# First pointwise product of a Conformer layer: eight column groups advanced together with the adaLN slices, and most of the depthwise convolution placed behind them

## The chip, the cores and the metric

The kernel runs on one core of a Trainium2 chip. The metric is device time in microseconds (us), the median of three runs. A core has a matrix engine (PE, TensorE), a vector engine (DVE), a scalar engine (ACT), a general engine (POOL) and a queue engine (SP) that here issues nearly every DMA. They run side by side, each in its own program order, and wait for each other by semaphores.

## The reference, cut to what matters

Two layers over x of 256 tokens by 2048 channels, all in 32-bit floats. Layer 0 mixes tokens by a Conformer convolution, layer 1 by differential attention, and each is followed by a squared-ReLU MLP (2048 to 8192 to 2048). Only the beginning of layer 0 is touched:

```
mod = silu(c) @ ada_w[0] + ada_b[0]         # (2048) @ (2048, 6 * 2048): sh_m, sc_m, g_m, sh_f, sc_f, g_f
h = x * (1 + sc_m) + sh_m
u = h @ pw1_w + b1                          # (256, 2048) @ (2048, 4096)
u = u[:, :2048] * sigmoid(u[:, 2048:])      # GLU
u = causal depthwise convolution of u, width 31, + b_dw
u = silu(layer_norm(u))                     # over the 2048 channels
y = u @ pw2_w + b2                          # (256, 2048) @ (2048, 2048)
x = layer_norm(alpha * x + g_m * y)
...
```

The channel h[:, k] needs sc_m[k] and sh_m[k], so the first product can't begin its contraction before the modulation vectors are there, and each of those six vectors costs the reading of a 2048 by 2048 block of ada_w (16 MB).

## The kernel before

**Products.** A product takes three PE matmuls for each 128 rows of contraction ("kc", 16 of them), 128 tokens and 512 columns: both operands are split into a high and a low part, and high x high, high x low and low x high are added in PSUM (`mm_parts`, L480; L488 to L490, and L563 to L566 in the later products). A weight tile of 1 MB is loaded, then split in two halves of 128x1024 each: ACT writes the high part (L476, L527), DVE the low part (L477, L528; a few on POOL). One half feeds 12 matmuls. PSUM has eight banks of 128x512: four for products (`mm_bank`), three for transposes and small things (`tp_tile`), one for the adaLN products.

**adaLN vectors.** There are two ways to compute one. The DVE way (`ada_slice_dve_steps`, L222) multiplies each row block of a loaded 1 MB tile with one column of silu(c) and adds it up (L248); matmuls with a vector of ones (L231) sum over the partitions. The PE way (`ada_slice_steps`, L264) multiplies on PE (L289; eight short matmuls for a 1 MB tile), copies, transposes (L272) and reduces. A step is one 1 MB tile.

**First part, L870 to L1001.** sc_m (DVE way) and sh_m (PE way) are computed in five slices of the 2048 channels, `SLICES` = 2, 4, 4, 4 and 2 blocks of 128. When a slice is there, h is transposed, scaled and split for its channels (`end_ada`, L934), and the first product advances over these kc for four of its eight column groups (a group is 512 columns: 256 of the value half and 256 of the gate half). Groups 0 and 1 (`RES`) stay in four PSUM banks for the whole time. Groups 2 and 3 (`ROT`) use rotating banks, and `add_up` (L942) adds each slice to a sum in SBUF. In between `ada_pair` works off one step of each kind for the next slice and loads two more tiles. PE, DVE, ACT and SP follow the order of the code here.

**Second part, L1055 to L1085.** Groups 4 to 7 run one after the other over all 16 kc (eight halves each). After each half `run_plan` issues what is due of the convolution: for each group j `glu` (L796), `conv_shift` (L742: 16 copies into a buffer in which the 31 taps become a contraction), `conv_taps`, `conv_products` (L763: 64 short matmuls for each of two channel blocks), `conv_out`, `conv_tok` and `conv_stats`. The convolution of groups 0 to 6 lies in this part; that of group 7 comes behind it. 24 of the 32 DVE steps for G_M and SC_F (8 channel blocks each) are spread over the 32 halves, with tiles loaded ahead (`dve_loads`).

**Third part, L1087 to L1138.** Group 7's convolution, PE steps of SH_F (`fill`), channel LayerNorm, swish.

**Fourth part, the second pointwise product "pw2"** (`out_proj`, L1202): 16 weight tiles. After each `pump_t2` (L1183) works off the remaining 8 DVE steps and the remaining PE steps of the 16 for SH_F. The PE steps' tiles are loaded ahead (`load_pe`, L376). For these last 8 DVE steps no load was issued ahead: `step` (L251) finds no tile and issues the load itself, right in front of its own arithmetic. DVE follows the order of the code from here on too (`early_ve`), and so its splits of the weights (L528) queue behind these steps. Then comes the MLP of layer 0.

Tiles for adaLN live in a pool of two buffers (`araw`), in halves of the buffer `ux`, and in the first part in two of the four buffers of the weight tiles (`ada_raw`, L193).

Of the kernel before, what the change touches and what calls it, by code (L numbers as in the profile page):

```python
# [19 lines left out]
P = 128  # L20
# [10 lines left out]
RES = (0, 1)  # L31
ROT = (2, 3)
ACC0 = 2
SLICES = ((0, 2), (2, 4), (6, 4), (10, 4), (14, 2))
ADA_T1 = 24
FILL = (2, 1, 1, 2)
# [17 lines left out]
OV_AT = 1  # L54
SUM_WAIT = 4
# [4 lines left out]
SHIFT = ("act", "act", "act", "dve")  # L60
END_ACT = (0, 3, 6, 9, 12, 15)
CONV_AT = (4, 8, 12, 16, 20, 24, 28)
# [16 lines left out]
def trunk(  # L79
# [68 lines left out]
    small_rows = {}  # L148

    def load_small(n, name, vs):  # L150
        o = 0
        for v in vs:
            r = vec_rows(v)
            nc.sync.dma_start(vtok[o:o + r.shape[0], 1, n * P:(n + 1) * P], r)
            o += r.shape[0]
        small_rows[name] = vtok[:o, 1, n * P:(n + 1) * P]
# [36 lines left out]
    def ada_raw(name, first):  # L193
        if pe_turn[0] > 0:
            if pe_turn[0] % 3 == 0:
                return ux[:, 2048:]
        elif first:
            n_raw[0] += 1
            n = n_raw[0] % 6
            if n in (2, 3):  # L200
                return ux[:, (n - 2) * 2048:(n - 1) * 2048]
            if n in (4, 5):
                return wraw.tile([P, 2048], F32, tag="raw", name=name)
        return araw.tile([P, 2048], F32, tag="araw", name=name)

    n_raw, pe_turn = [0], [0]
    ux = big.tile([P, 4096], F32, tag="uTh", name="conv_ux")

    def slice_tiles(i, v, f0, nf, first):

        n0, w = (v * KC + f0) * P, nf * P
        per = 2048 // w
        av = ada_w[i].rearrange("(kc p) n -> p kc n", p=P)

        def load(a):
            t = ada_raw(f"aw_{i}_{v}_{f0}_{a}", first)
            tv = t.rearrange("p (j n) -> p j n", n=w)
            nc.sync.dma_start(tv, av[:, per * a:per * (a + 1), n0:n0 + w])
            return tv
        return load, per, w  # L220

    def ada_slice_dve_steps(i, v, f0, nf, m, first=True):  # L222
# [3 lines left out]
        load, per, w = slice_tiles(i, v, f0, nf, first)  # L226
# [37 lines left out]
    def ada_slice_steps(i, v, f0, nf, m, first=False, apart=False):  # L264

        st = {}
        load, per, w = slice_tiles(i, v, f0, nf, first)
# [74 lines left out]
    ada_q, dve_loads, dve_q, pe_q = [], [], [], []  # L342

    def add_dve(v, f0, m):
        loads, steps = ada_slice_dve_steps(0, v, f0, 8, m, False)
        dve_loads.extend(loads)
        dve_q.extend(steps)
    m_gm, m_scf, m_shf = mod_tile(0, G_M), mod_tile(0, SC_F), mod_tile(0, SH_F)
    add_dve(G_M, 0, m_gm)
    add_dve(G_M, 8, m_gm)  # L350
    add_dve(SC_F, 0, m_scf)
    add_dve(SC_F, 8, m_scf)
    pe_loads = []
    for f0 in range(0, KC, 4):
        loads, steps = ada_slice_steps(0, SH_F, f0, 4, m_shf, apart=True)
        pe_loads.extend(loads)
        pe_q.extend(steps)
# [10 lines left out]

    def pump_early(q, n=1):
        for _ in range(n):  # L370
            if q:
                q.pop(0)()
                if q is pe_q:
                    load_pe()

    def load_pe():  # L376
        if pe_loads:
            pe_turn[0] = 1 - pe_turn[0]
            pe_loads.pop(0)()
            pe_turn[0] = -pe_turn[0]  # L380
# [350 lines left out]
    xs_buf = [ux[:, 0:4 * 2 * UW], econv.tile([P, 4 * 2 * UW], F32, name="conv_x")]  # L731
# [8 lines left out]
    turn = {j: n for n, j in enumerate(ROT + RES + tuple(range(len(RES + ROT), 8)))}  # L740

    def conv_shift(j, bs=range(4)):  # L742

        u = cs[j]["u"].rearrange("p n s -> p (n s)")
        for b in bs:
            for r in range(4):
                dst, src = xs_buf[turn[j] % 2][32 * r:32 * r + 32, b, :XW], u[32 * b:32 * b + 32, r:r + XW]
                if (4 * b + r in END_ACT) if j == 7 else SHIFT[(r - b) % 4] == "act":
                    nc.scalar.copy(dst, src)
                else:  # L750
                    nc.vector.tensor_copy(dst, src)

    def conv_taps(j, n):
        cs[j]["dg", n] = []
        for hb in range(2):
            w = work.tile([P, 16, 32], F32, tag="CB"[n], name=f"conv_w_{j}_{n}_{hb}")
# [6 lines left out]
    def conv_products(j, n):  # L763
        cs[j]["ps", n] = ps = tp_tile(f"cv_{j}_{n}")
        for k4 in range(8):
            for b in range(4):
                nc.tensor.matmul(ps[32 * b:32 * b + 32, :S], lhsT=cs[j]["dg", n][k4 // 4][:, (k4 % 4) * 4 + b, :],
                                 rhs=xs_buf[turn[j] % 2][:, b, n * UW + 4 * k4:n * UW + 4 * k4 + S],
# [20 lines left out]
    def glu_copy(j, pss):  # L789
        cs[j]["ut"] = []  # L790
        for t in range(NT):
            u_t = work.tile([P, NG], F32, tag="A", name=f"utok_{j}_{t}")
            nc.scalar.copy(u_t, pss[t])
            cs[j]["ut"].append(u_t)

    def glu(j):  # L796
        ut = cs[j]["ut"]
        if turn[j] < len(u_buf):
            u = u_buf[turn[j]]
        else:  # L800
            u = work.tile([P, 2, UW], F32, tag="X", name=f"u_{j}", bufs=3)
        cs[j]["u"] = u
        pa = tp_tile(f"pa_{j}")
        pg = tp_tile(f"pg_{j}")
# [21 lines left out]
    pss0 = {g: [mm_bank(f"pw1_{g}_ps{t}") for t in range(NT)] for g in RES}  # L826
    accs = {g: [vtok[:, t, (ACC0 + r) * NG:(ACC0 + r + 1) * NG] for t in range(NT)] for r, g in enumerate(ROT)}
# [53 lines left out]
    order = [ROT + RES if nf == 2 else tuple(g for gs in zip(ROT, RES) for g in gs) for f0, nf in SLICES]  # L881
    n_first = len(RES + ROT)
    w_src = [(f"pw1_{g}_{s}", pw1v[:, f0:f0 + nf, :, g * 256:(g + 4 // nf) * 256])
             for s, (f0, nf) in enumerate(SLICES) for g in order[s][::4 // nf]]
    w_src += [(f"pw1_{g}_{i}", pw1v[:, i:i + 4, :, g * 256:(g + 1) * 256])
              for g in range(n_first, 8) for i in range(0, KC, 4)]
# [47 lines left out]
    def end_ada(s):  # L934
        f0, nf = SLICES[s]
        for f in ada_end[s]:
            f()
        nc.vector.tensor_scalar(mul[:, f0:f0 + nf], m_sc[:, f0:f0 + nf], 1.0, None, ALU.add)
        to_featT(z, hT, mul, m_sh, "h0", range(f0 // 2, (f0 + nf) // 2))()
        later.extend([lambda q=q: alpha_x(q) for q in range(f0 // 4, (f0 + nf) // 4)])  # L940

    def add_up(g, s, pss):  # L942
        for t in range(NT):
            if s == 0:
                nc.scalar.copy(accs[g][t], pss[t])
            else:
                nc.vector.tensor_tensor(accs[g][t], accs[g][t], pss[t], op=ALU.add)
# [5 lines left out]
    for _ in range(2):  # L953
        load_w()
    for _ in range(2):
        ada_load.pop(0)()
# [9 lines left out]
    for s, (f0, nf) in enumerate(SLICES):  # L966
        last = f0 + nf == KC
        n_half = nf // 2 * n_first
        nxt = 0 if last else len(ada_step[s + 1])
        pair_at = {4: (0, 1, 2, 3) if n_half == 4 else (1, 3, 5, 7), 2: (2, 4), 0: ()}[nxt]  # L970
        h = 0
        for n, g in enumerate(order[s]):
            pss = pss0[g] if g in RES else [tp_tile(f"pw1_{g}_{s}_ps{t}") for t in range(NT)]
            k0, k1 = (0, KC - 1) if g in RES else (f0, f0 + nf - 1)
            for q in range(nf // 2):
                split_half()
                mm_parts(pss, hT, w_parts.pop(0), f0 + 2 * q, k0, k1)
                pending()
                if h in pair_at:
                    ada_pair(s + 1)  # L980
                if nxt and h == (5 if nxt == 2 else n_half - 1):
                    pending()
                    end_ada(s + 1)
                h += 1
            if g in ROT:
                later.append(lambda g=g, s=s, pss=pss: add_up(g, s, pss))
                cs[g]["ut"] = accs[g]
                if nf == 2:
                    pending()
            if last and n == 2:  # L990
                glu(ROT[0])
                glu_copy(RES[0], pss0[RES[0]])
        if s == CV_AT:
            conv_vectors()
        if s == OV_AT:
            load_small(1, "adab1", [ada_b[1]])
            load_small(2, "b1", [mlp_b1[0], mlp_b1[1]])
        if s == OV_AT + 1:
            load_small(3, "ln", [ln_mix_g[0], ln_mix_b[0], ln_ffn_g[0], ln_ffn_b[0], ln_mix_g[1], ln_mix_b[1]])
            load_small(0, "subg", [attn_subln_g[0]])  # L1000
    pending()  # L1001
# [22 lines left out]
    pairs = sorted(turn, key=turn.get)  # L1024
    for n, c in enumerate(CONV_AT):
        for e in range(2):
            at(c + 2 * e + 2, conv_tok, pairs[n], e)
            at(c + 2 * e, conv_products, pairs[n], e)
    at(1, glu, pairs[1])
    at(5, glu, pairs[2])  # L1030
    at(9, glu, pairs[3])
    at(13, glu, pairs[4])
    at(17, glu, pairs[5])
    at(25, glu, pairs[6])
    for n, c in enumerate(CONV_AT):
        for e in range(2):
            at(c + 2 * e + 1, conv_out, pairs[n], e)
            at(max(0, c + 2 * e - 3), conv_taps, pairs[n], e)
            at(c + 2 * e + 3, conv_stats, pairs[n], e)
        for b in range(4):  # L1040
            at(c - 4 + b if n < 6 else (c - 3, c - 2, c - 2, c - 1)[b], conv_shift, pairs[n], [b])
    pw1 = {}
    at(6, lambda: glu_copy(pairs[3], pss0[pairs[3]]))
    at(10, lambda: glu_copy(4, pw1[4]))
# [550 lines left out]
```

## Time and profile before

| | |
|---|---|
| median of 3 runs | 2450.39 us (2448.82 to 2453.74) |
| profiled execution: time | 2448.23 us |
| profiled execution: span from first to last instruction | 2446.4 us |
| PE busy / DVE busy / ACT busy | 2302.1 / 1764.3 / 1064.3 us |
| mean granted PE clock | 0.97 |
| bytes moved by DMA | 608.5 MB |
| first matmul of pw1 / last matmul of pw1 | 33.0 / 359.5 us |
| first matmul of pw2 / last matmul of pw2 | 398.6 / 532.5 us |
| first matmul of the MLP | 547.0 us |

How to read the lines: a row of the stretches ("windows") gives start and end, its length, the busy time of PE, PE's weight loads, DVE, ACT and POOL with the number of instructions, and then the granted PE clock (1.00 is full), the DMA share and GB/s. A row of the groups gives line, engine, operation, tiles, shapes and count, then busy us and mean ns of one, and then the idle time before them and what ended it. A row of the waits gives who waited for whom, us in total, times, longest. A row of the timeline gives start and duration. PE matmuls overlap, so that the pace of PE is the distance between two starts, not the duration of one, and a "busy" PE can be a slow one.

### The profile page before, as it was taken

The numbers are of one execution on the slowest core, as the hardware profiler recorded it, in microseconds if no ns is written. First come the engines' busy times: TensorE is split into PE (matmuls) and PEld (weight loads), VectorE is DVE, ScalarE is ACT, GpSimd is POOL, SyncE is SP. The second block draws the span as 40 slices with busy tenths as digits, with TensorE's granted clock in tenths as the row PEclk, the third lists the DMA queues.
The fourth block names the chain that finished last, engine by engine and source line by source line (L and its number), as shares of the span: only waits on it lengthen the run. The fifth ranks groups of instructions, "written<-read, shape, count | busy, mean of one in ns | idle before, by whom it ended". The sixth has DMA issues, their size and how long they took to land.

```text
span 2446.4 us, 28510 instructions
## 1 busy us (share of the span) xinstructions
PE 2302.1 (94%) x11167; PEld 1829.7 (75%) x11167; DVE 1764.3 (72%) x1988; ACT 1064.3 (44%) x1370; POOL 245.7 (10%) x162
## 2 busy tenths in 40 slices
PE   4898988789999999999998999998999999999997
PEld 2666664567778888888886888886788888888886
DVE  5667873578898878878868777787877665565566
ACT  2336654234434434434435454444543443443442
POOL 0000000122060000000004300012204000000002
PEclk9889998899999999999998999999999999999999
DMA  9976776667889888888874676686686555556563
GB/s 350 349 249 235 256 249 249 231 241 262 323 301 330 288 318 303 293 311 306 302 257 160 228 243 222 227 288 211 217 286 217 188 189 189 191 188 194 185 223 103
DMA packets 274027, 608.53 MB, mean 249 GB/s; under 512 B 11038, under 2 KB 48484, under 8 KB 260580
## 3 DMA queue, kind: packets, MB, share of 16 engines
q1 hardware_dynamic: 273652, 606.41, 72.0%
q8 instruction: 87, 1.43, 0.2%
q10 hardware_dynamic: 240, 0.30, 0.1%
q14 instruction: 48, 0.39, 0.0%
HBM read 604.54 MB, written 2.13 MB: 248 GB/s over the span
## 4 chain that ended last, share of the span: by engine, by line
PE 70%; issue 18%; DVE 7%; DMA 3%; ACT 1%; POOL 1%; DVEq 0%; ACTq 0%; POOLq 0%; SPq 0%
PE w_ps L563 17%; PE w_ps L566 17%; PE w_ps L565 17%; DVE wl_w L528 1%; PE qkv_q_ps L566 1%; PE qkv_q_ps L565 1%; PE qkv_q_ps L563 1%; PE qkv_v_ps L566 1%; PE qkv_v_ps L563 1%; PE qkv_v_ps L565 1%; DMA w_w<-in_mlp_w_dram 1%; PE qkv_k_ps L566 1%; PE qkv_k_ps L563 1%; PE qkv_k_ps L565 1%; PE pw_ps L563 1%
## 5 line engine op out<-in xcount | busy, mean ns | idle before, releaser
L528 DVE TENSOR_TENSOR wl_w<-w_w,wh_w 128x1024 fp32r<-128x1024 f32 x502 | 632.9, 1279 | 333.3 <-ACT wh_w L527 333.0
L527 ACT CAST wh_w<-w_w 128x1024 fp32r<-128x1024 f32 x512 | 537.6, 1053 | 758.1 <-PE w_ps L566 573.7
L563 PE MATMUL w_ps<-wh_w,hm_hi 128*128 128x512 f32 x1024 | 403.3, 394 | 4.5 <-ACT hm_hi L396 4.5
L565 PE MATMUL w_ps<-wl_w,hm_hi 128*128 128x512 f32 x1024 | 400.1, 391 | 4.9 <-DVE wl_w L528 4.8
L565 PE MATMUL w_ps<-wl_w,u_hi 128*128 128x512 f32 x1024 | 399.6, 390 | 5.2 <-DVE wl_w L528 5.2
L566 PE MATMUL w_ps<-wh_w,hm_lo 128*128 128x512 f32 x1024 | 400.1, 391 | 0.9 <-DVE hm_lo L399 0.9
L563 PE MATMUL w_ps<-wh_w,u_hi 128*128 128x512 f32 x1024 | 400.5, 391 | 0.0
L566 PE MATMUL w_ps<-wh_w,u_lo 128*128 128x512 f32 x1024 | 399.2, 390 | 0.0
L315 DVE SCALAR_TENSOR_TENSOR acc<-adaw,cond,acc 128x2048 f32<-128x2048 f32 (+1 forms) x105 | 244.5, 2328 | 0.8 <-DMA adaw<-in_ada_w_dram 0.6
L563 PEld LDWEIGHTS w_ps<-wh_w,hm_hi 128*128 128x128 f32 x1024 | 193.0, 189 | 49.3 <-ACT hm_hi L396 6.2
L565 PEld LDWEIGHTS w_ps<-wl_w,hm_hi 128*128 128x128 f32 x1024 | 193.0, 189 | 45.9 <-DVE wl_w L528 6.9
L565 PEld LDWEIGHTS w_ps<-wl_w,u_hi 128*128 128x128 f32 x1024 | 192.6, 188 | 46.4 <-DVE wl_w L528 7.0
L566 PEld LDWEIGHTS w_ps<-wh_w,hm_lo 128*128 128x128 f32 x1024 | 192.7, 188 | 42.7 <-DVE hm_lo L399 2.5
L563 PEld LDWEIGHTS w_ps<-wh_w,u_hi 128*128 128x128 f32 x1024 | 192.6, 188 | 42.4 <-issue 2.5
L566 PEld LDWEIGHTS w_ps<-wh_w,u_lo 128*128 128x128 f32 x1024 | 192.6, 188 | 40.0
L248 DVE SCALAR_TENSOR_TENSOR aacc<-aw,cond,aacc 128x1024 f32<-128x1024 f32 (+2 forms) x112 | 112.1, 1001 | 48.7 <-DMA aw<-in_ada_w_dram 46.2
L528 POOL TENSOR_TENSOR wl_w<-w_w,wh_w 128x1024 fp32r<-128x1024 f32 x10 | 24.0, 2406 | 1095.7 <-ACT wh_w L527 1095.7
L488 PE MATMUL pw_ps<-wh_pw,h_hi 128*128 128x512 f32 x256 | 108.7, 424 | 10.7 <-ACT h_hi L396 10.6
L477 DVE TENSOR_TENSOR wl_pw<-w_pw,wh_pw 128x1024 fp32r<-128x1024 f32 x64 | 78.0, 1223 | 47.9 <-ACT wh_pw L476 47.3
L489 PE MATMUL pw_ps<-wl_pw,h_hi 128*128 128x512 f32 x256 | 103.8, 405 | 0.7 <-DVE wl_pw L477 0.7
L490 PE MATMUL pw_ps<-wh_pw,h_lo 128*128 128x512 f32 x256 | 103.6, 405 | 0.0
L476 ACT CAST wh_pw<-w_pw 128x1024 fp32r<-128x1024 f32 x64 | 66.2, 1048 | 46.0 <-DMA w_pw<-in_conv_pw_w_dram 36.2
(337 smaller groups left out, 3220.6 us busy)
## 6 DMA issues: line engine op xcount, KB each, us to landing
w_w<-in_mlp_w_dram SPq DMA_DIRECT2D x256, 1024.0 KB, 5.5
adaw<-in_ada_w_dram SPq DMA_DIRECT2D x96, 1024.0 KB, 5.9
aw<-in_ada_w_dram SPq DMA_DIRECT2D x68, 1024.0 KB, 7.2
w_pw<-in_conv_pw_w_dram SPq DMA_DIRECT2D x64, 512.0 KB, 5.9
conv_ux<-in_ada_w_dram SPq DMA_DIRECT2D x16, 1024.0 KB, 12.6
w_pw<-in_conv_pw_w_dram SPq DMA_DIRECT2D x16, 1024.0 KB, 5.5
w_qkv_q<-in_attn_qkv_w_dram SPq DMA_DIRECT2D x16, 1024.0 KB, 5.1
w_qkv_k<-in_attn_qkv_w_dram SPq DMA_DIRECT2D x16, 1024.0 KB, 5.0
```

What stands on the lines that cost most here:

```text
L248: nc.vector.scalar_tensor_tensor(st["acc"], wv[:, kc % per, :], cond[:, kc:kc + 1], st["acc"], ALU.mult, ALU.add)
L315: nc.vector.scalar_tensor_tensor(st["acc"], w, cond[:, kc:kc + 1], st["acc"], ALU.mult, ALU.add)
L476: nc.scalar.copy(hq, rq)
L477: nc.vector.tensor_tensor(lq, rq, hq.bitcast(F32), op=ALU.subtract)
L488: nc.tensor.matmul(pss[t], lhsT=xh, rhs=wh, start=(kc == first), stop=False)
L489: nc.tensor.matmul(pss[t], lhsT=xh, rhs=wl, start=False, stop=False)
L490: nc.tensor.matmul(pss[t], lhsT=xl, rhs=wh, start=False, stop=(kc == last))
L527: nc.scalar.copy(hi, rq)
L528: eng.tensor_tensor(lo, rq, hi.bitcast(F32), op=ALU.subtract)
L563: nc.tensor.matmul(pss[tt], lhsT=xh, rhs=wh, start=(kc == 0 and job["bias"] is None), stop=False)
L565: nc.tensor.matmul(pss[tt], lhsT=xh, rhs=wl, start=False, stop=False)
L566: nc.tensor.matmul(pss[tt], lhsT=xl, rhs=wh, start=False, stop=(kc == nk - 1))
```

## The change

The first product advances in all eight column groups with each slice of sc_m and sh_m. `SLICES` is now 2, 2, 4, 4 and 4 blocks. No group stays in PSUM: each takes two rotating banks for a slice, and `add_up` copies (first slice, ACT) or adds (the other four, DVE) both 128x512 results to sums in SBUF. The adaLN tiles of the first part have five buffers of their own (two of `araw`, two halves of `ux`, the new `conv_x`), and the weight tiles keep their four. `end_ada` and the making of h (`put_h`, two channel blocks at a time) are called some halves before the slice's products end (`END_AT`).

The convolution of groups 0 and 1 is interleaved with the products of the last slice (16 halves); that of groups 2 to 7 follows behind, in 12 steps, each with one step of adaLN: `ADA_CONV` = DPDDPDDPDDPD, so 8 DVE steps and 4 PE steps. 10 of 16 shift copies are ACT's and 6 DVE's for every group (before, 12 and 4, for group 7 6 and 10). GLU's transposes use `mm_bank`.

G_M (second half) and SH_F (second half) go the PE way, G_M (first half), SC_F and SH_F (first half) the DVE way: 32 DVE steps and 16 PE steps as before, in one sequence `ada_seq`. `ada_next` works off one step and then loads the tile of the step four places on, so that four tiles are loaded or loading at any time. 12 steps lie in the convolution, 6 PE steps in the fills, and the remaining 30 (24 DVE, 6 PE) in pw2.

```diff
-SLICES = ((0, 2), (2, 4), (6, 4), (10, 4), (14, 2))
-ADA_T1 = 24
-FILL = (2, 1, 1, 2)
+NGRP = 8
+SLICES = ((0, 2), (2, 2), (4, 4), (8, 4), (12, 4))
+PAIR_AT = ((1, 3), (0, 2, 3, 5), (1, 4, 7, 10), (1, 4, 7, 10), ())
+END_AT = (5, 6, 12, 12, None)
+STAGE = ((9, 11), (13, 15), (16, 17), (18, 19), (20, 21), (22, 23), (24, 25), (26, 27))
+ADA_CONV = "DPDDPDDPDDPD"
+FILL = (1, 1, 2, 2)
...
+        homes = {"first": ("own", "own", ux[:, :2048], ux[:, 2048:], conv_x[:, :2048]),
+                 "conv": ("own", "weights"), "pw2": ("own", ux[:, 2048:], "own", conv_x[:, :2048])}[n_raw[1]]
...
+    add_later("D", G_M, 0, m_gm)
+    add_later("P", G_M, 8, m_gm)
+    add_later("D", SC_F, 0, m_scf)
+    add_later("D", SC_F, 8, m_scf)
+    add_later("D", SH_F, 0, m_shf)
+    add_later("P", SH_F, 8, m_shf)
+    ada_seq = []
+    for e in ADA_CONV + "P" * sum(FILL) + "DDDDP" * 8:
+        if later_ada[e]:
+            ada_seq.append(later_ada[e].pop(0))
...
+    def ada_ahead():
+        if ada_seq:
+            load, step = ada_seq.pop(0)
+            load()
+            ahead.append(step)
+
+    def ada_next(n=1):
+        for _ in range(n):
+            if ahead:
+                ahead.pop(0)()
+                ada_ahead()
...
     def add_up(g, s, pss):
         for t in range(NT):
             if s == 0:
-                nc.scalar.copy(accs[g][t], pss[t])
+                nc.scalar.copy(cs[g]["ut"][t], pss[t])
             else:
-                nc.vector.tensor_tensor(accs[g][t], accs[g][t], pss[t], op=ALU.add)
+                nc.vector.tensor_tensor(cs[g]["ut"][t], cs[g]["ut"][t], pss[t], op=ALU.add)
...
     for s, (f0, nf) in enumerate(SLICES):
         last = f0 + nf == KC
...
         h = 0
...
+        for g in range(NGRP):
+            pss = [mm_bank(f"pw1_{g}_{s}_ps{t}") for t in range(NT)]
             for q in range(nf // 2):
                 split_half()
...
+                mm_parts(pss, hT, w_parts.pop(0), f0 + 2 * q, f0, f0 + nf - 1)
                 pending()
...
+                if h in PAIR_AT[s]:
                     ada_pair(s + 1)
...
+                if not last and h >= END_AT[s]:
+                    n = h - END_AT[s] - 1
+                    if n < 0:
+                        pending()
+                        end_ada(s + 1)
+                    elif n < SLICES[s + 1][1] // 2:
+                        put_h(s + 1, SLICES[s + 1][0] // 2 + n)
+                if last:
+                    run_plan(h)
+                    if h in (2, 8, 9, 10):
+                        if h == 2:
+                            n_raw[:] = [0, "conv"]
+                        ada_ahead()
                 h += 1
+            later.append(lambda g=g, s=s, pss=pss: add_up(g, s, pss))
...
+    for n in range(len(ADA_CONV)):
+        run_plan(16 + n)
+        ada_next()
+        tick()
...
     def pump_t2():
         n_t2[0] += 1
         if n_t2[0] == 1:
-            n_t2.extend([len(dve_q), len(pe_q)])
-        for q, n in ((dve_q, n_t2[1]), (pe_q, n_t2[2])):
-            while len(q) > max(0, n * (1 - n_t2[0] / ADA_T2)):
-                pump_early(q)
+            n_t2.append(len(ahead) + len(ada_seq))
+        while len(ahead) + len(ada_seq) > max(0, n_t2[1] * (1 - n_t2[0] / ADA_T2)):
+            ada_next()
```

The loop `for g in range(n_first, 8)` of the second part is removed.

More of the change, by code (lines that the diff above doesn't have):

```diff
@@ L148, in trunk @@
     small_rows = {}
+    rows_sb = work.tile([P, NG], F32, tag="bc_b2", name="small_rows", bufs=1)
     def load_small(n, name, vs):
@@ L225, in ada_slice_dve_steps @@
         st = {}
-        load, per, w = slice_tiles(i, v, f0, nf, first)
+        load, per, w = slice_tiles(i, v, f0, nf)
         def finish():
@@ L266, in ada_slice_steps @@
         st = {}
-        load, per, w = slice_tiles(i, v, f0, nf, first)
+        load, per, w = slice_tiles(i, v, f0, nf)
         def finish():
@@ L787, in conv_stats @@
             nc.vector.bn_stats(vst[t][:, ch, :], vtok[:, t, ch * P:(ch + 1) * P])
[L789 to L794, printed above, removed]
     def glu(j):
         ut = cs[j]["ut"]
[L798 to L801, printed above, removed]
+        u = u_buf[j % 3]
         cs[j]["u"] = u
-        pa = tp_tile(f"pa_{j}")
-        pg = tp_tile(f"pg_{j}")
+        pa = mm_bank(f"pa_{j}")
+        pg = mm_bank(f"pg_{j}")
         for cc in range(2):
@@ L965, in trunk @@
     end_ada(0)
[L966 to L1001, printed above, removed]
+    put_h(0, 0)
     gate0 = {}
@@ L1101, in trunk @@
[L1101 to L1104 removed]
+    assert not plan
     mv = small.tile([P, NT, 2], F32, tag="cmv", name="cln_mv", bufs=1)
```

228 lines of the change are left out of this document (94 added, 134 removed).

## The prediction

> **What bounds the kernel now.** I first cut the beginning into stretches at the first and last products of each part.
>
> ```profile
> 0.00:33.00 33.00, 7.96 (x48) 4.16 (x48) 13.70 (x33) 9.57 (x20) 1.98 (x11) 1.00 0.96 326
> 33.00:120.00 87.00, 73.86 (x317) 50.26 (x318) 57.23 (x80) 28.05 (x36) 0.00 (x0) 0.84 1.02 357
> 120.00:183.00 63.00, 57.05 (x270) 43.66 (x269) 42.40 (x68) 20.56 (x28) 0.00 (x0) 0.89 0.78 251
> 183.00:360.00 177.00, 163.50 (x1399) 116.01 (x1398) 140.65 (x196) 110.79 (x170) 0.00 (x0) 0.97 0.72 242
> 360.00:398.00 38.00, 28.02 (x247) 12.90 (x247) 15.15 (x39) 18.14 (x33) 0.72 (x1) 0.81 0.83 296
> 398.00:533.00 135.00, 116.94 (x504) 85.00 (x502) 72.82 (x76) 41.10 (x48) 21.92 (x9) 0.90 0.70 246
> 533.00:547.00 14.00, 6.64 (x32) 2.76 (x32) 13.69 (x22) 6.89 (x14) 7.77 (x5) 0.66 0.26 80
> ```
>
> PE looks busy everywhere, so I went to its timeline for the pace: the distance between two starts in pw2, once at full clock and once in a throttled stretch.
>
> ```profile
> 530.25 0.39 PE L565 MATMUL pw_ps<-wl_pw,swish_hi 128*128 128x512 f32 x1
> 530.48 0.39 PE L566 MATMUL pw_ps<-wh_pw,swish_lo 128*128 128x512 f32 x1
> ...
> 402.73 0.63 PE L563 MATMUL pw_ps<-wh_pw,swish_hi 128*128 128x512 f32 x1
> 403.16 0.63 PE L565 MATMUL pw_ps<-wl_pw,swish_hi 128*128 128x512 f32 x1
> ```
>
> A matmul costs 0.23 us at full clock and 0.43 throttled. The first product has 16 kc x 8 groups x 2 x 3 = 768, so 177 us of PE at full clock; half of it, 88 us, is all that 33 to 183 has to do besides short adaLN work, in 150 us. There the DMA share is 1.02 at 357 GB/s until 120: 32 MB of ada_w stand against only 16 MB of weights, and PE waits for the modulation. The waits of PE from 25 to 200 say the same at each slice's end, and those in pw2 (395 to 545) show another cause:
>
> ```profile
> PE apt L231 <- DVE aacc L248: 11.2, 4, 4.7
> PE pw_ps L488 <- ACT h_hi L396: 10.6, 4, 7.6
> ...
> DVE aacc L248 <- DMA aw<-in_ada_w_dram: 46.2, 6, 16.3
> PE pw_ps L565 <- DVE wl_pw L528: 18.0, 3, 8.2
> DVE aacc L246 <- DMA aw<-in_ada_w_dram: 11.0, 1, 11.0
> ```
>
> In pw2 DVE stands 57.2 us still in front of the 8 DVE steps whose tiles were not loaded ahead. The splits queue behind them, and PE behind the splits: pw2 has 384 matmuls, 88 us, and takes 135 at a granted clock of 0.90.
>
> **The first part, slice by slice.** The durations that I use; the last four rows are a PE step of 1 MB, the first and the last of the eight transposes of a GLU, and the 64 matmuls of one `conv_products`:
>
> ```profile
> L477 DVE TENSOR_TENSOR wl_pw<-w_pw,wh_pw 128x1024 fp32r<-128x1024 f32 x64 | 78.0, 1223 | 47.9 <-ACT wh_pw L476 47.3
> L947 DVE TENSOR_TENSOR vtok<-vtok,pw_ps 128x512 f32<-128x512 f32 x16 | 10.4, 682 | 1.6 <-PE pw_ps L490 1.6
> L248 DVE SCALAR_TENSOR_TENSOR aacc<-aw,cond,aacc 128x512 f32<-128x512 f32 x30 | 22.5, 750 | 0.7
> L399 DVE TENSOR_TENSOR h_lo<-h_h,h_hi 128x512 fp32r<-128x512 f32 x8 | 5.5, 692 | 10.2 <-ACT h_hi L396 10.2
> L423 DVE TENSOR_SCALAR h_h<-h_t,h_mul,mod 128x256 f32<-128x256 f32 x8 | 4.3, 541 | 2.1 <-PE h_t L414 2.0
> ...
> 383.51 1.07 PE L289 MATMUL aps<-aw,condr 128*32 128x512 f32 x8
> ...
> 279.41 0.27 PE L808 MATMUL pa<-ident,utok 128*128 128x128 f32 x1
> 280.18 0.27 PE L809 MATMUL pg<-ident,utok 128*128 128x128 f32 x1
> 283.35 3.66 PE L767 MATMUL cv<-conv_x,conv_w 128*32 128x256 f32 x64
> ```
>
> The first product of the kernel stays at 33 us: the same four ada_w tiles, x and weight tile come ahead of it, the two more weight tiles behind them. A half is 12 x 0.23 = 2.76 us of PE.
> Slice 0: 8 halves 22, two PE steps 2, and 3 because PE began at half pace: 27 us.
> Slice 1: DVE is longer than PE's 22. 8 splits x 1.22 = 9.8, 16 adds x 0.68 = 10.9, 16 rows for slice 2 x 0.75 = 12, h 1.2: 34. Its modulation ends only at its last halves (END_AT 6 of 8), so one handover stays open; before, four handovers cost 11.2 + 10.6 us, so 5.5 each. 40 us. DMA doesn't bind: by its end 16 ada_w tiles, x and about 9 weight tiles are needed, 27 x 1.05 MB, 79 us at 357 GB/s, and the sum stands at 100.
> Slices 2 and 3: PE 16 x 2.76 = 44.2, four PE steps 4.3, transposes and sums 3: 51.5. DVE 16 x 1.22 + 16 x 0.68 + 12 + 2.5 = 45. DMA 8 + 8 tiles of 1.05 MB at 357 GB/s 47. PE bounds, and the handover lies 3 halves ahead; I add 3 us: 54.5 each, 109 for both.
> Slice 4 loads no modulation: 44.2, four conv_products 14.6, four GLU transposes 4 x 1.05 (279.41 to 280.45), 5 for DVE adds that free the banks which GLU takes (0.68 or 1.36 each): 68 us.
> Sum 244, so pw1 ends at 277, against 359.5, but with two groups convolved where before seven were and 24 DVE steps done. The adds are 64 instead of 16, 33 us more of DVE, and I cost them at nothing in slices 2 to 4 since PE's time there covers DVE's, by 6.5 us in slices 2 and 3; without that cover each further microsecond of DVE would count. ACT's copies out of PSUM come to the same number: 12 for the sums of the first slice come in, 12 in front of GLU go.
>
> **The convolution behind it.** Six groups and 12 adaLN steps, 8 of them on DVE:
>
> ```profile
> L751 DVE COPY conv_x<-u 32x571 f32<-32x571 f32 x18 | 8.1, 450 | 0.4
> L757 DVE TENSOR_TENSOR conv_w<-eye,wct 128x512 f32<-128x512 f32 x32 | 20.4, 681 | 0.0
> L787 DVE BATCH_NORM_STATS2 vst<-vtok 128x6 f32<-128x128 f32 x32 | 7.6, 282 | 12.4 <-ACT vtok L782 12.4
> L818 DVE SCALAR_TENSOR_TENSOR u<-pa,cols_conv,sg 128x256 f32<-128x256 f32 x10 | 4.4, 479 | 7.2 <-ACT sg L816 7.2
> L749 ACT COPY conv_x<-u 32x571 f32<-32x571 f32 x30 | 20.0, 667 | 1.4 <-DVE u L818 1.0
> L773 ACT ACTIVATE vpe<-cv,cols_conv 128x256 f32<-128x256 f32 x16 | 7.6, 472 | 19.3 <-PE cv L767 19.3
> L782 ACT COPY vtok<-vt 128x256 f32<-128x256 f32 x16 | 5.8, 369 | 11.9 <-PE vt L780 11.9
> L816 ACT ACTIVATE sg<-pg,cols_conv 128x256 f32<-128x256 f32 x16 | 6.7, 471 | 40.7 <-PE pg L809 40.7
> 443.29 2.60 DVE L248 SCALAR_TENSOR_TENSOR aacc<-aw,cond,aacc 128x1024 f32<-128x1024 f32 x2 [10.32 <-DMA aw<-in_ada_w_dram]
> ```
>
> For one group DVE needs 6 x 0.45 + 4 x 0.68 + 4 x 0.28 + 2 x 0.48 + 1.33 steps x 2.60 = 11.0 us; ACT 10 x 0.667 + 2 x (0.47 + 0.47 + 0.37) = 9.3; PE 2 x 3.66 + 1.05 + 0.4 + 0.67 x 1.07 = 9.5. The shift copies of a group are issued a stage earlier than its products, so the three overlap. DVE leads: 6 x 11.0 = 66, and 6 for waits between engines so evenly loaded: 72. The 12 MB need 35 us at 357 GB/s and are requested four ahead. This ends at 349.
>
> From the last conv product to the first of pw2 the old trace takes 380 to 398.6; at the end of it three PE steps wait for tiles. With tiles four ahead I take 15 of these 18.6 us. pw2 then starts at **364 instead of 398.6**.
>
> **pw2.** 16 more DVE steps come in here, behind which the splits queue. DVE: the old 72.8 us + 16 x 2.60 = 114.4 us. SP now carries 30 ada_w tiles less 4 loaded, and 16 weight tiles less 4: 38 x 1.05 = 40 MB, 112 us at 357 GB/s; at 246 GB/s, this stretch before, it would be 162. PE: 88 + 6 steps 6.4 + sums, about 100. What disappears is the 57.2 us wait, if loads four ahead cover it. The two bounds of 112 and 114 lie so close that I add 12%: 128 us, against 135. The old DVE time is no lower end, as 72.8 contains everything but the 16 steps; 114 is one, 162 the other, and I stay near the lower since loads were late there for want of requests, not of bandwidth. A page of the Trainium skill, Perfetto Trace Analysis, section Engine Utilization, puts the ceiling of a lone core's 16 DMA engines at about 435 GB/s; by it the 40 MB would take an estimated 92 us and DVE alone would bound. No stretch quoted here passes 357.
>
> Last product of pw2: 364 + 128 = 492 instead of 533. Nothing behind it is changed, and the modulation of the MLP is drained by the same tile as before. **41 us less.** The profiled execution took 2448.2 us, 1.8 more than its span, and the median of the runs is 2450.4, 2.2 above it. I take the difference from the median: **2409 us**.
>
> **Rivals.**
> *Waits replaced nothing (slower).* The 24 DVE steps of pw2 keep a wait for their tile, because SP takes requests in order: an ada_w load that waits for its buffer holds the weight loads behind it. For: DVE waited 57.2 / 8 = 7.2 us per step, and 40 MB in 114 us are 351 GB/s, about what the fullest stretch moved. Against: those loads were issued with no lead. With w us a step, pw2 takes 114 + 24 w; it passes 533 - 364 = 169 from w = 2.3 us on. At half the old wait, 3.6, it takes 200, and the kernel 2450 + 31 = 2481.
> *The clock.* Products now change banks every 12 or 24 matmuls; each change waits for DVE, PE pauses, and the clock falls. The row 33 to 120 was granted 0.84; if that held through the slices, their PE work of 177 + 14 steps x 1.07 + 14.6 + 4.2 = 211 us would take 251, with 19 us of waits on top 270 instead of 244: 2435. Speaking against: until 120 PE waited for DMA, and from 183 the clock was 0.97. The Trainium skill, TensorE: Matmul & The Clock Gate, section A second HAM failure mode: psum-queue depth-cycling, describes just such pauses when groups cycle through PSUM banks. The trace of before bears it out only where DMA waits stand beside it.
> *The convolution runs in series.* If shift copies and products don't overlap, a group takes GLU 1.05 + 0.94 + 0.96, ACT's copies 6.7, products 7.3 = 17 us; 6 x 17 = 102 instead of 72: 2439.
> *No waits at all.* Without the 19 us of waits in the slices, the 6 in the convolution and the 14 in pw2: 2370.
> *It doesn't do what it says.* If DMA still paces the slices, 8 + 8 tiles each at the 313 GB/s to which the rows from 33 to 183 average (357 x 87 and 251 x 63 over 150) take 54 us, no more than the 54.5 that I have; so this leaves the time as it is.
>
> **How the numbers follow.** Forecast 0.50 (2390 to 2430); no waits 0.14; clock 0.12; series 0.09; slower by pw2's waits 0.15. A difference under 0.2%, about 5 us, can't be told from none. Faster takes the forecast, no waits and 0.15 of the clock and series cases, 0.79; the remaining 0.06 of these is the same. The range, 2377 to 2456: its lower end leaves out a third of the no-waits case, its upper end most of the slower one.
>
> **What would show it.** In the profile after: pw1's last matmul near 277, pw2's first near 364, its last near 492. Right for the first part: the granted clock above 0.9 and DMA below full from 100 on, and PE's waits on L231 and h_hi well under 21.8 us. Right for pw2: DVE's wait for aw near nothing and DVE busy over 85%. Wrong: that wait above 24 x 2.3 = 55 us, or stretches in which the clock falls at the end of each group.

## The result, and the profile after

The changed kernel takes 2414.5 us (median of four runs, 2409.88 to 2417.51), against 2450.39 before: a ratio of 0.985, with a 95% interval of 0.9823 to 0.9876. A fourth run of the kernel before took 5037.51 us and is left out of that ratio. The profiled execution has a span of 2414.5 us against 2446.4, so 31.9 us less. The prediction said 41 less and 2409 us.

I cut the trace of after at the same kinds of points as that of before: pw1 from 33 to 271, the convolution to 341, the fills to 357, pw2 to 502.

```profile
33.00:120.00 87.00, 76.54 (x355) 54.35 (x354) 62.61 (x93) 35.93 (x50) 0.00 (x0) 0.94 0.98 340
120.00:183.00 63.00, 62.69 (x302) 46.21 (x301) 53.79 (x72) 24.33 (x27) 0.00 (x0) 1.00 0.97 329
183.00:271.00 88.00, 85.86 (x551) 66.68 (x553) 65.94 (x112) 45.98 (x65) 0.00 (x0) 1.00 0.44 148
271.00:341.00 70.00, 66.52 (x966) 36.01 (x966) 60.44 (x124) 53.83 (x98) 0.72 (x1) 0.98 0.58 209
341.00:357.00 16.00, 8.41 (x44) 3.32 (x45) 5.33 (x10) 9.66 (x16) 0.00 (x0) 0.79 1.04 393
357.00:502.00 145.00, 122.46 (x521) 89.54 (x520) 119.28 (x110) 41.31 (x49) 22.39 (x9) 0.88 0.96 358
```

In the slices the granted clock (third number from the right) rose from 0.84 and 0.89 to 0.94 and 1.00. In pw2 DMA went from 0.70 to 0.96 of full, and DVE's busy time from 72.8 to 119.3 us. The view by tile gives the ends of each part (minimum, median and maximum of one in ns, then first and last start in us); the rows are the last of the three products in pw1, and the last and the first in pw2:

```profile
L495 PE MATMUL pw_ps<-wh_pw,h_lo x256: 387/389/628, 33.6 to 270.4; 128*128 128x512 f32 x128
L571 PE MATMUL pw_ps<-wh_pw,swish_lo x128: 387/389/628, 357.2 to 502.1; 128*128 128x512 f32 x128
L568 PE MATMUL pw_ps<-wh_pw,swish_hi x128: 389/389/796, 356.7 to 501.6; 128*128 128x512 f32 x128
```

pw1 ends 89 us earlier (270.4 for 359.5). From there to pw2's first product it takes 86 us instead of 39, since six groups of the convolution now lie here. So pw2 starts 42 us earlier (356.7 for 398.6). It then lasts 145 us instead of 134, and gives 11.5 of the 42 back. Behind pw2 nothing moved: 2414.5 - 502.1 = 1912.4 us, before 2446.4 - 532.5 = 1913.9.

The waits of the slices (25 to 300), in the columns who, for whom, us in total, times, longest:

```profile
PE pw_ps L493 <- ACT h_hi L401: 9.3, 3, 7.6
...
PE apt L231 <- DVE aacc L248: 1.5, 1, 1.5
```

PE's wait for the modulation sums fell from 11.2 to 1.5 us. The wait for the new h seems hardly to fall, from 10.6 to 9.3, but 7.6 us of both are the wait in front of the very first product, before and after:

```profile
33.02 0.80 PE L488 MATMUL pw_ps<-wh_pw,h_hi 128*128 128x512 f32 x1 [7.64 <-ACT h_hi L396]
32.54 0.79 PE L493 MATMUL pw_ps<-wh_pw,h_hi 128*128 128x512 f32 x1 [7.64 <-ACT h_hi L401]
```

Between slices PE thus waited 3.0 us for h before and 1.7 after. And the waits of pw2 (357 to 502):

```profile
PE aps L289 <- DMA aw<-in_ada_w_dram: 10.0, 2, 6.0
...
PE aps L289 <- DMA conv_x<-in_ada_w_dram: 5.1, 2, 4.8
DVE aacc L246 <- DMA aw<-in_ada_w_dram: 3.6, 1, 3.6
...
PE aps L289 <- DMA conv_ux<-in_ada_w_dram: 2.9, 1, 2.9
...
DVE aacc L248 <- DMA aw<-in_ada_w_dram: 1.1, 1, 1.1
```

DVE's 57.2 us of waiting for tiles are down to 4.7. In its place PE waits 18.0 us for the tiles of its own adaLN steps. What DMA carried meanwhile (counts of transfers, KB each, median us to landing):

```profile
DMA packets 20170, 51.97 MB, mean 358 GB/s; under 512 B 832, under 2 KB 848, under 8 KB 20037
...
aw<-in_ada_w_dram SPq DMA_DIRECT2D x15, 1024.0 KB, 12.0
w_pw<-in_conv_pw_w_dram SPq DMA_DIRECT2D x11, 1024.0 KB, 10.3
conv_x<-in_ada_w_dram SPq DMA_DIRECT2D x8, 1024.0 KB, 8.3
conv_ux<-in_ada_w_dram SPq DMA_DIRECT2D x7, 1024.0 KB
w_w<-in_mlp_w_dram SPq DMA_DIRECT2D x4, 1024.0 KB, 5.2
conv_ux<-gb_d SPq DMA_DIRECT2D x1, 1024.0 KB
```

These are 15 + 8 + 7 = 30 adaLN tiles, 11 weight tiles, 4 for the MLP and one of the gate, in 52 MB, where the prediction had counted 40. Four of the 30 adaLN tiles are not of the 48 of `ada_seq`: they belong to the next vector, G_F (`gf_load`).

### The profile page after: what moved, and what is told of

The parts are those of the page before. It is cut to its first block, busy times and chain, and to the rows that moved or that the text cites. A ratio compares the mean times of both kernels' runs of the same rounds, so it can differ in the third digit from the quotient of the medians.

```text
span 2414.5 us, 28618 instructions
## 1 busy us (share of the span) xinstructions
PE 2287.4 (95%) x11167; PEld 1820.8 (75%) x11167; DVE 1803.1 (75%) x2046; ACT 1057.5 (44%) x1360; POOL 247.9 (10%) x162
## 4 chain that ended last, share of the span: by engine, by line
PE 77%; DVE 11%; DMA 5%; issue 3%; ACT 3%; SPq 1%; POOL 1%; DVEq 0%; ACTq 0%; POOLq 0%
PE w_ps L568 18%; PE w_ps L571 18%; PE w_ps L570 18%; DVE aacc L248 2%; DMA aw<-in_ada_w_dram 2%; PE pw_ps L493 2%; PE pw_ps L494 2%; PE pw_ps L495 2%; PE cv L771 2%; DVE wl_w L533 1%; PE qkv_q_ps L571 1%; PE aps L289 1%; PE qkv_q_ps L570 1%; PE qkv_q_ps L568 1%; PE qkv_v_ps L571 1%
## 5 line engine op out<-in xcount | busy, mean ns | idle before, releaser
L493 PE MATMUL pw_ps<-wh_pw,h_hi 128*128 128x512 f32 x256 | 106.1, 414 | 12.1 <-ACT h_hi L401 9.3
L248 DVE SCALAR_TENSOR_TENSOR aacc<-aw,cond,aacc 128x1024 f32<-128x1024 f32 (+2 forms) x70 | 75.8, 1083 | 2.8 <-DMA aw<-in_ada_w_dram 1.1
## 6 DMA issues: line engine op xcount, KB each, us to landing
w_pw<-in_conv_pw_w_dram SPq DMA_DIRECT2D x16, 1024.0 KB, 10.5
```

What stands on the lines that cost most here:

```text
L248: nc.vector.scalar_tensor_tensor(st["acc"], wv[:, kc % per, :], cond[:, kc:kc + 1], st["acc"], ALU.mult, ALU.add)
L493: nc.tensor.matmul(pss[t], lhsT=xh, rhs=wh, start=(kc == first), stop=False)
```

## The experiments

Two questions were open. Which of the two full resources holds pw2, DVE with its 16 further steps or DMA with its 52 MB? And what made the part before it 42 us shorter: fewer bytes ahead of each slice, earlier handovers, or something else? Where the expectations use letters, these are short for the theories: A and B for the two about pw2, C for the bytes ahead of the slices and D for another cause there. Ratios are to the kernel before, run on the same chip. In three of the kernels below only earlier parts were edited, and their pw2 lasted 140, 140.5 and 144 us; the changed kernel's own was 145. So a pw2 of 140 to 145 counts here as unchanged.

### pw2 without half of its adaLN loads

```diff
-            nc.sync.dma_start(tv, av[:, per * a:per * (a + 1), n0:n0 + w])
+            if n_raw[1] != "pw2" or n_raw[0] % 2:
+                nc.sync.dma_start(tv, av[:, per * a:per * (a + 1), n0:n0 + w])
```

> The changed kernel with every second adaLN load of pw2 left out (15 of 30 tiles, 15.7 MB; the steps run on what the buffer holds, so the modulation is wrong). Theory A, DMA paces pw2 (52 MB at 358 GB/s are the whole 145 us): pw2 falls from 145 to near its DVE busy time of 119, the kernel to about 2392. Theory B, DVE paces it (24 steps, some stretched beside POOL, with the splits queued behind them): pw2 stays within 5 us of 145, the kernel within 5 us of 2414.

Measured: 2407.28 us, ratio 0.9826 (0.9811 to 0.9841). The windows of this kernel, pw2:

```profile
352.00:492.00 140.00, 121.28 (x525) 90.84 (x524) 121.34 (x111) 41.59 (x50) 24.18 (x9) 0.90 0.71 254
```

DMA is free for nearly a third of the time, and pw2 still takes 140 us, inside the scatter. What was gained is pw2's start, 5 us earlier; the first of the loads left out are issued ahead of it. So DMA alone isn't the bound: DVE, 121.3 of 140 us busy, is close behind. PE's waits say so too. For adaLN tiles it waits 7.6 us here instead of 18.0, but for DVE's sums longer, 10.2 us instead of 4.6:

```profile
PE apt L232 <- DVE aacc L249: 10.2, 2, 5.6
```

### pw2 without half of DVE's adaLN rows

```diff
-            for kc in range(a * per, (a + 1) * per):
+            for kc in range(a * per, (a + 1) * per - (n_raw[1] == "pw2")):
                 row(kc)
-            if kc == KC - 1:
+            if a == KC // per - 1:
```

> The changed kernel with one of the two rows of each DVE step in pw2 left out (half the terms of these sums are missing), all loads kept: 24 x 1.3 = 31 us less of DVE. Theory A, DMA paces: pw2 stays within 5 us of 145. Theory B, DVE paces: pw2 falls by 25 us or more, the kernel to about 2390.

Measured: 2406.41 us, ratio 0.9827 (0.9812 to 0.9842). pw2 in this kernel's windows:

```profile
357.00:490.00 133.00, 117.64 (x522) 86.17 (x522) 84.77 (x86) 41.37 (x49) 20.82 (x9) 0.91 1.02 386
```

DVE's work falls by 34.5 us, and pw2 by 7 to 12. Now DMA is at 1.02 of full with 386 GB/s. So DVE alone isn't the bound either.

### Both left out

The two edits above together.

> The changed kernel with both edits at once: every second adaLN load of pw2 and one of the two rows of its DVE steps left out (so the modulation is wrong). Alone they took 5 and 13 us out of pw2's 145. If DMA and DVE are two bounds that lie close, each hiding the other, both together take pw2 to about 110, the 111 that the kernel before reached with its loads ahead: 30 us or more. If something else holds it, such as PE's waits for the tiles of its own adaLN steps, it stays above 125.

Measured: 2381.72 us, ratio 0.9732 (0.9716 to 0.9748). pw2 in its windows:

```profile
351.00:466.00 115.00, 111.00 (x525) 83.05 (x525) 85.31 (x87) 41.74 (x50) 20.92 (x9) 0.99 0.85 310
```

Here pw2 takes 115 us at a clock of 0.99, 25 to 30 less than unchanged, where the two edits alone made 0 to 5 and 7 to 12. Measured at the end of pw2, they bring its last product forward by 10.6 and 12.1 us alone (502.1 to 491.5 and 490.0), and by 36.6 together (465.5). By the ratios the kernel gains about 6, 6 and 29 us on the changed one, and the interval of either edit alone overlaps with that of the changed kernel. Two bounds stand a few microseconds apart (133 us with DVE's work lowered, 140 with DMA's), and each hides the other.

Not all of the 30 us from 145 to 115 is waiting. PE's idle time falls by 18.5 us (from 22.5 to 4.0), and its busy time by 11.5 (122.5 to 111.0), at a granted clock of 0.88 and 0.99. What the clock alone would give wasn't separated.

### DVE's splits kept off POOL

In the trace of after, some pairs of DVE's adaLN rows last nearly twice as long as others. DVE's timeline in pw2 (start, duration):

```profile
408.56 2.60 DVE L248 SCALAR_TENSOR_TENSOR aacc<-conv_ux,cond,aacc 128x1024 f32<-128x1024 f32 x2
...
412.29 4.74 DVE L248 SCALAR_TENSOR_TENSOR aacc<-aw,cond,aacc 128x1024 f32<-128x1024 f32 x2
```

and POOL's in the same stretch:

```profile
411.60 3.03 POOL L533 TENSOR_TENSOR wl_pw<-w_pw,wh_pw 128x1024 fp32r<-128x1024 f32 x1 [9.80 <-ACT wh_pw L532]
```

The long pair lies on top of a split that POOL does. The Trainium skill, SBUF — State Buffer, section SBUF: two separate sides, says that a DVE operation with two inputs in SBUF and a POOL operation that reads SBUF take one shared pair of ports in turn, each for its whole instruction; the 2.60 and 4.74 us agree with that.

```diff
-POOL_T2 = ((5,),(2,5),(2,5),())
+POOL_T2 = ((),(),(),())
```

> The changed kernel with pw2's five split halves of the table POOL_T2 given back from POOL to DVE: 6 us more of work on DVE, but the five DVE steps that took 4.6 to 4.7 us beside POOL should take 2.6, 10 us less. Theory A, DMA paces: no change beyond 3 us. Theory B, DVE paces: about 4 us less, if the stretch is due to POOL.

Measured: 2411.19 us, ratio 0.9849 (0.9832 to 0.9865). The groups of pw2 in the changed kernel (count, busy us, mean ns of one, idle time before):

```profile
L248 DVE SCALAR_TENSOR_TENSOR aacc<-aw,cond,aacc 128x1024 f32<-128x1024 f32 x21 | 35.1, 1671 | 1.7 <-DMA aw<-in_ada_w_dram 1.1
```

and in this one:

```profile
L248 DVE SCALAR_TENSOR_TENSOR aacc<-aw,cond,aacc 128x1024 f32<-128x1024 f32 x21 | 29.0, 1381 | 1.7 <-DMA aw<-in_ada_w_dram 1.1
```

The stretching is real, 6 us in these rows, but DVE gets five splits of 1.2 us back. pw2 takes 137 us, a little below the scatter; the total can't be told from the changed kernel's.

### The old kernel with fewer bytes in its slices

The kernel before, with 9 of the 32 adaLN tiles of the first part not loaded.

```diff
-            nc.sync.dma_start(tv, av[:, per * a:per * (a + 1), n0:n0 + w])
+            if not (first and n_raw[0] > 6 and n_raw[0] % 6 in (2, 3)):
+                nc.sync.dma_start(tv, av[:, per * a:per * (a + 1), n0:n0 + w])
```

> The kernel before with 9 of the 32 adaLN tiles of its slices not loaded (9.4 MB; the steps run on what the buffer holds, so the modulation is wrong), all instructions kept. Theory C, DMA paced the old slices: the part from 33 to 183 us shrinks by up to 9.4 MB at 357 GB/s, 26 us, less what handovers and other waits keep: 15 to 26. Rival D, the old slices were paced by their handovers (21.8 us of PE waits) and by buffers that adaLN and weight tiles shared: under 5 us.

Measured: 2433.19 us, ratio 0.9943 (0.9924 to 0.9961). Its slices in the windows:

```profile
33.00:183.00 150.00, 138.21 (x654) 100.22 (x655) 111.36 (x164) 62.82 (x84) 0.00 (x0) 0.93 0.83 278
```

and pw1's last product by tile:

```profile
L491 PE MATMUL pw_ps<-wh_pw,h_lo x256: 387/389/628, 33.9 to 344.3; 128*128 128x512 f32 x128
```

pw1 ends 15 us earlier (344.3 for 359.5), and pw2 starts 15 earlier (383.7 for 398.6). Some of this can be scatter: in the kernel with its last loads issued ahead (below), whose slices are unedited, pw1 ends at 353.5. The h of the last slice is made at 152.4 us here, at 167.2 in the kernel before and at 164.5 in that other one, so 12 to 15 us were won in the slices. 9.4 MB at the 357 GB/s that the kernel before moved from 33 to 120 are 26 us, so about half of what the bytes cost was on the path. The old slices were paced by DMA, though not by DMA alone.

### The changed kernel with fewer bytes in its slices

The same in the changed kernel, 10 of 32 tiles.

```diff
-            nc.sync.dma_start(tv, av[:, per * a:per * (a + 1), n0:n0 + w])
+            if not (n_raw[1] == "first" and n_raw[0] > 5 and n_raw[0] % 5 in (3, 4)):
+                nc.sync.dma_start(tv, av[:, per * a:per * (a + 1), n0:n0 + w])
```

> The changed kernel with 10 of the 32 adaLN tiles of its slices not loaded (10.5 MB), all instructions kept. Theory C says that PE paces its slices now, but for the second one: 5 us or less. If DMA still paced them: about 28 us.

Measured: 2410.99 us, ratio 0.9859 (0.9835 to 0.9882). pw1's last product in this kernel:

```profile
L496 PE MATMUL pw_ps<-wh_pw,h_lo x256: 387/389/628, 33.4 to 264.9; 128*128 128x512 f32 x128
```

10.5 MB less bring 5.5 us (264.9 for 270.4), though the DMA share in the slices of the changed kernel is 0.98 and 0.97 until 183. All of it lies in the second slice, shown here for the changed kernel and for this one:

```profile
61.00:98.00 37.00, 29.65 (x131) 19.45 (x131) 28.30 (x40) 11.62 (x16) 0.00 (x0) 0.89 1.07 373
61.00:93.00 32.00, 25.82 (x126) 16.98 (x127) 27.60 (x37) 11.45 (x16) 0.00 (x0) 1.00 0.71 236
```

So DMA, at 373 GB/s, held the second slice in part. The slices behind it last 54, 53 and 66 us in the changed kernel and 54, 53 and 65 here, although the DMA share of the third falls from 0.93 to 0.80. A share near 1 says that transfers are under way, not that somebody waits for them. PE paces these later slices.

### The handovers between slices made late

```diff
-END_AT = (5, 6, 12, 12, None)
+END_AT = (7, 7, 15, 15, None)
```

> The changed kernel with the end of the modulation and the making of h put back to the last half of each slice (END_AT 7, 7, 15, 15), so that PE waits for them at each slice's end. By the 5.5 us per handover of the prediction three handovers come back, 11 to 16 us: about 2428. Rival D, that the early handover is what the change gained in its first part: 30 us or more.

Measured: 2424.12 us, ratio 0.9906 (0.9884 to 0.9927). PE's wait for h in this kernel, 25 to 280:

```profile
PE pw_ps L493 <- ACT h_hi L401: 17.9, 5, 7.6
```

The wait goes from 9.3 to 17.9 us, pw1 ends 10.7 later (281.1) and pw2 starts 10.9 later (367.6). So handing over one to three halves earlier is worth 11 us.

### The adds of two slices left out

```diff
-            else:
+            elif s not in (2, 3):
                 nc.vector.tensor_tensor(cs[g]["ut"][t], cs[g]["ut"][t], pss[t], op=ALU.add)
```

> The changed kernel with the adds of slices 2 and 3 left out (32 x 0.68 = 22 us of DVE; half of the contraction is missing from the first product). The prediction costs them at nothing since PE paces these slices: pw1 ends within 2 us of 270. If DVE, or banks that wait for its adds, paced them: 10 to 22 us earlier.

Measured: 2415.1 us, ratio 0.9864 (0.9849 to 0.988). pw1's last product starts at 270.0 instead of 270.4. 32 adds of 0.68 us, 22 us of DVE, cost nothing in these two slices.

### The old kernel with its last loads issued ahead

The kernel before, with the 8 remaining DVE tiles of pw2 loaded one step ahead into the buffer of the shift copies. Nothing else of the change is in it.

```diff
+        elif late_d[0]:
+            return conv_x[:, :2048]
...
                 q.pop(0)()
                 if q is pe_q:
                     load_pe()
+                elif dve_loads:
+                    dve_loads.pop(0)()
+                    late_d[0] = bool(dve_loads)
...
+    late_d[0] = True
+    dve_loads.pop(0)()
```

> The kernel before with one edit: each of the last 8 DVE steps has its tile loaded one step ahead, into the buffer that the convolution has left. If the missing lead was what held pw2, DVE's 57 us of waiting go, pw2 falls from 135 to about 105 and the kernel to about 2420, with no regrouping at all. Rival: the tiles come late for want of bandwidth or behind other requests on SP, and less than 10 us go.

Measured: 2426.45 us, ratio 0.9918 (0.9902 to 0.9934). pw2 in its windows:

```profile
396.00:507.00 111.00, 111.00 (x502) 81.98 (x501) 66.27 (x72) 40.84 (x48) 22.22 (x9) 0.96 0.82 287
```

The 57.2 us wait is gone, pw2 takes 111 us instead of 134, and the kernel 20 us less. More than half of what the whole change brings was to be had by one load of lead. The span fell by 18.9 us where pw2's end moved by 25.2. The MLP's first product follows pw2's last by 14.2 us here and by 14.5 before, so the other 6 us lie in the part behind, which the edit doesn't touch: 1920 us from pw2's end here, 1910 to 1917 in the other kernels.

### Four, then eight, adaLN steps moved into the last slice

The last slice has room: between 205 and 271 the changed kernel's windows show DMA at 0.38.

```profile
205.00:271.00 66.00, 63.86 (x442) 49.21 (x444) 51.51 (x91) 39.25 (x57) 0.00 (x0) 1.00 0.38 128
```

The edit starts the loads ahead at halves 0, 1, 12 and 14, and works off four DVE steps there, so that pw2 has four less:

```diff
+ADA_LAST = "DDDD"
+LAST_AT = (5, 8, 11, 14)
...
-    for e in ADA_CONV + "P" * sum(FILL) + "DDDDP" * 8:
+    for e in ADA_LAST + ADA_CONV + "P" * sum(FILL) + "DDDDP" * 8:
...
-                    if h in (2, 8, 9, 10):
-                        if h == 2:
+                    if h in (0, 1, 12, 14):
+                        if h == 0:
                             n_raw[:] = [0, "conv"]
                         ada_ahead()
+                    if h in LAST_AT:
+                        ada_next()
```

The buffers that the tiles take in turn are set accordingly, and the two halves of SC_F change places.

> A version: four of the DVE steps move from pw2 into the last slice, where DMA moved only 128 GB/s and DVE was busy 51.5 of 66 us (10.4 us more makes 62). Theory A: pw2 loses 4.2 MB, 12 us. Theory B: pw2 loses 10.4 us. In both the last slice may grow by up to 4 us: 2402 to 2408. If DVE turns out to pace the last slice, the slice grows by 10 and nothing is gained.

Measured: 2408.68 us, ratio 0.9834 (0.9816 to 0.9852). Its windows, last slice and pw2:

```profile
205.00:270.00 65.00, 61.91 (x429) 47.32 (x427) 56.13 (x91) 39.25 (x57) 0.00 (x0) 1.00 0.43 146
358.00:486.00 128.00, 114.79 (x523) 85.14 (x522) 106.98 (x102) 41.22 (x49) 21.90 (x9) 0.95 1.00 375
```

The last slice isn't longer, and pw2 is 12 to 17 us shorter. The second version adds the POOL edit to it:

```diff
-POOL_T2 = ((5,),(2,5),(2,5),())
+POOL_T2 = ((),(),(),())
```

> The version with four DVE steps in the last slice, and pw2's five split halves given back from POOL to DVE. DVE steps beside POOL took 4.6 us instead of 2.6: with that gone, pw2's stretch 3 to 8 us shorter than the 128 of the version; if DMA alone holds it now (375 GB/s), no difference.

Measured: 2405.21 us, ratio 0.9825 (0.981 to 0.9839). pw2 is again 128 us:

```profile
361.00:489.00 128.00, 116.77 (x525) 86.42 (x525) 103.31 (x106) 41.84 (x50) 7.71 (x4) 0.93 1.00 376
```

With DMA at 1.00 in both, less work on DVE buys no more there. The third moves eight steps instead of the first version's four, half of them PE's:

```diff
-ADA_LAST = "DDDD"
-LAST_AT = (5, 8, 11, 14)
+ADA_LAST = "PDPDPDPD"
+LAST_AT = (3, 5, 7, 9, 11, 12, 13, 15)
...
                     if h in LAST_AT:
                         ada_next()
+                        tick(2)
```

> A version with eight adaLN steps in the last slice, four on PE and four on DVE: 8.4 MB less in pw2 than in the changed kernel, and four steps of 1.07 us more on PE, which paces that slice. The slice 4 to 7 us longer, pw2 at 115 to 122, the kernel 2396 to 2404. If PE waits there for late tiles (two buffers only), the slice grows by 10 or more and nothing is gained over the version with four.

Measured: 2404.73 us, ratio 0.9821 (0.9807 to 0.9836). Its windows:

```profile
205.00:276.00 71.00, 66.31 (x460) 48.08 (x460) 55.54 (x95) 39.77 (x58) 0.00 (x0) 0.98 0.57 193
366.00:493.00 127.00, 112.17 (x486) 86.09 (x486) 109.69 (x98) 40.03 (x47) 23.76 (x9) 0.93 0.94 346
```

Four PE steps more make the last slice 6 us longer, pw1 ends at 276.4, and pw2 stays at 127, where 115 to 122 were expected. In it PE waits 6.3 us for an adaLN tile, 4.3 for DVE's splits and 4.2 for its sums; what holds it at 127 isn't settled. By their ratios the three versions lie 0.2 to 0.3% below the changed kernel, but their intervals overlap with its 0.9823 to 0.9876; that any of them is faster isn't shown.

## Why the prediction held, point by point

**The total** is 5.5 us off, and part of that closeness is luck. pw2 started 7 us before the forecast (356.7 for 364) and took 17 more, so its end is 10 us late (502.1 for 492). The medians then differ by 35.9 us where the profiled spans differ by 31.9.

**The slices** came out nearly as worked: sum 244 predicted, 270.4 - 32.5 = 238 measured; one by one 28, 37, 54, 53 and 66 us for 27, 40, 54.5, 54.5 and 68. The experiments with fewer bytes show that DMA held 12 to 15 us of the old slices, and that PE paces the last three of the new ones. The second slice came near its number for another reason than the one given: DVE was to hold it and DMA not to bind, but DVE is busy for 28.3 of its 37 us, and fewer bytes make it 5 us shorter. The handovers were costed too high. The 5.5 us for each counted in the 7.6 us in front of the first product; without these the four of the kernel before cost 11.2 + 3.0 = 14.2 us, 3.5 each. In the changed kernel PE waited 1.5 + 1.7 = 3.2 us in all, where some 11.5 were allowed. The adds at nothing: shown for the third and fourth slice. One sign was wrong: DMA was to be below full from 100 on, and its share stayed at 0.97 until 183. The conclusion held without it.

**The clock** as a rival is refuted: 1.00 from 120 to 271, while products change banks every 24 matmuls, and 1.00 in the first slice, where they change every 12:

```profile
33.00:61.00 28.00, 26.60 (x138) 20.27 (x137) 17.64 (x30) 14.99 (x23) 0.00 (x0) 1.00 1.07 369
```

The second slice, which changes every 12 too, was granted 0.89, but 1.00 in the kernel with fewer bytes, so the changes weren't what lowered it. The Trainium skill's failure mode (TensorE: Matmul & The Clock Gate, section A second HAM failure mode: psum-queue depth-cycling) didn't appear at this pace.

**The convolution** was predicted at 72 us and the way to pw2's first product at 15. By tile, the last of its bulk's products starts at 333.7, so 63 and then 23. The sum is right (86 for 87), but by luck, as two errors cancel in it: the groups overlapped better than I allowed, and the way to pw2 didn't get shorter than the old 18.6. PE still waits 6.5 us for adaLN tiles in it (5.6 before), with DMA full; in the kernel without half of pw2's adaLN loads this wait is gone, and the way takes 17.7 us (333.8 to 351.5). The end of it in the changed kernel:

```profile
341.00:357.00 16.00, 8.41 (x44) 3.32 (x45) 5.33 (x10) 9.66 (x16) 0.00 (x0) 0.79 1.04 393
```

The rival of a convolution in series, 102 us, is refuted.

**pw2 is the term that was mis-sized**: 128 predicted, 145 measured (140 to 145 over kernels with the same pw2). The step that failed reads: "SP now carries 30 ada_w tiles less 4 loaded, and 16 weight tiles less 4: 38 x 1.05 = 40 MB". The 26 adaLN tiles of it are right. The whole trace has 84 of these loads, 32 for the slices, 48 of `ada_seq` and 4 for G_F:

```profile
L218 SPq DMA_DIRECT2D aw<-in_ada_w_dram x48: 367/398/2834, 1.2 to 487.6; - x48
L218 SPq DMA_DIRECT2D conv_ux<-in_ada_w_dram x21: 367/421/4487, 2.3 to 484.9; - x21
L218 SPq DMA_DIRECT2D conv_x<-in_ada_w_dram x15: 367/368/2576, 25.3 to 485.4; - x15
```

30 of them are issued from 357 on, so 54 before: the 32, the 18 steps that were worked off, and four ahead. What the step left out is what this stretch fetches besides: the 4 tiles of G_F, issued last, from 479 us on, 4 MLP tiles, a gate tile, and some 3.5 MB in flight from before. Together these are 52 MB, about 146 us at the prediction's own 357 GB/s, and 145 were measured. DVE's term, 114.4, measured 119.3; the stretching beside POOL, 6 us in the rows of that experiment, is of this size. The 12% for two close bounds wasn't what was too small: with either bound lowered pw2 takes 133 or 140 us, with both in place 140 to 145, and with both lowered 115.

**The slower rival** (DVE's steps keep a wait for their tiles) is refuted: 4.7 us for 24 steps is 0.2 a step, far under the 2.3 that it needed. The waits did come back, but at PE, 18.0 us.

**What stays open**: of the 42 us before pw2, 12 to 15 are shown to hang on bytes and 11 on early handovers, in kernels that aren't the same; the rest isn't separated. Nor was it tried to give the regrouped first part an old-style short pw2 of 111 us, by keeping more of the 30 steps out of it.

## What to carry to other kernels

When work moves between stages, count the bytes of each stage anew, with what is still in flight from the stage before and what the next one already fetches: 40 MB on paper were 52 here. Where two resources are within some 10% of each other, test them together before giving up on either: 0 to 5 and 7 to 12 us alone were 25 to 30 together. Before a wait is costed, look where in its window it lies: 7.6 of the 10.6 us of waiting for h stood in front of the first product and couldn't be won. And first give a late load one step of lead, since in an engine that works in order everything queues behind it: that alone was worth 20 us of the 36.

## What the runs showed of the hardware

DMA moved more than the 357 GB/s that was the most in the prediction: 386 GB/s over 133 us with half of DVE's rows left out, 393 in the row from 341 to 357 above. This lies between the pace at which I had costed pw2's tiles and the 435 GB/s that the Trainium skill gives as the ceiling of a lone core (Perfetto Trace Analysis, section Engine Utilization). And a pair of DVE's 128x1024 rows went from 2.60 to 4.74 us beside one POOL split of 3.03 us.
